# A whole network in one kernel: the first branches re-ordered with one logarithm, output projections taken by pairs of blocks, and priorities for the conformer's statistics

## The chip, the cores and the metric

The kernel runs on one core of a Trainium2 chip. The metric is the device time of one execution in microseconds (us). A core has five engines that each work through their own queue in order: TensorE (PE; its weight loads are shown apart as PEld), VectorE (DVE), ScalarE (ACT), GpSimd (POOL) and SyncE (SP), which here issues DMA transfers.

## The reference

One sequence of 256 tokens with 1024 features goes through two hybrid layers and then through a second stack: mixer, attention, FFN, conformer, attention, FFN. What is computed in the places of the change:

```python
def hybrid_layer(...):                       # twice, l = 0 and 1
    h = rms_norm(x, norm_pre);  proj = h @ w_in
    # sb_*, ml_*, gm_*, rt_*, xa_* and the gates are column blocks of proj
    y_sb = stick_breaking(sb_q, sb_k, sb_v)  # below
    q_ml = silu(causal_conv(ml_q, conv_q))   # k_ml likewise
    h_ml = mlstm(q_ml, k_ml, ml_v, ml_i + b_igate, ml_f + b_fgate)
    ...                                      # three more branches
    merged = sum(sigmoid(gates) * up(ys))
    return x + rms_norm(merged @ w_out, norm_post)

def stick_breaking(q, k, v):                 # by blocks of 128 queries, 4 heads
    z = q @ k.T * scale;  valid = key_pos < q_pos
    log_keep = where(valid, -softplus(z), 0)
    later = reverse_cumsum(log_keep) - log_keep
    return where(valid, exp(log_sigmoid(z) + later), 0) @ v

x = x + mixer_ab(x)      # ... concatenate([y_a, y_b]) @ w_out
x = x + cross_attn(x, mem, 0);  x = x + conv_ffn(x, 0)
def conformer_conv(x):
    h = glu(rms_norm_2(x) @ w1 + b1);  h = causal_dwconv(h, dw_w, dw_b)
    return silu(layer_norm_2(h)) @ w2 + b2
x = x + conformer_conv(x)
x = x + cross_attn(x, mem, 1);  x = x + conv_ffn(x, 1)
return rms_norm_2(x, final_norm)
```

## The kernel before, in words

Activations lie with features on partitions, in blocks of 128x256. Every matrix product is made in float32 from two halves, high and low: `wh*xh + wh*xl + wl*xh`. The weights stream from HBM in tiles of 512 KB (`weights`, L274 on): SP loads a tile `raw`, ScalarE rounds it to `wh` (L289), VectorE subtracts for `wl` (L290), and TensorE reads both. `raw` has five buffers, `wh` and `wl` four, so the conversion of a tile waits until TensorE is done with one four tiles back.

Three helpers issue the products. `mm_F` (L294) makes a feature-major block; its tiles in PSUM are named psF, or psO in an output projection. It goes over its 128-column blocks and, in each, over the four k-blocks of two weight tiles. `mm_T` makes token-major tiles psT, `proj_P` tiles psP. One weight tile is worth 24 matmuls of 128x256. `proj_F` (L339) calls `mm_F` in two steps of four k-blocks and may run a function `mid` between them.

A norm is applied late: `Norm.pair` adds squares (`sqacc`, L213 to L226) while it splits x into `xhl`; `column` sums over partitions with the matmul ps_ss (L169), `row_of` turns the result with ps_rb (L182) into a row that scales later outputs.

The order of a hybrid layer: projections sb_q and sb_k, with the statistic between; `blocks` makes the logits z of three blocks in turn, and `got` takes each at once through Exp (L557), Ln (L558), mask, and the halves sb_sp (L565, L566). Then sb_v, the gates' columns (`gates_if`), and sb_z, in whose middle `later` runs: eight matmuls ps_later (L578), Exp, mask on POOL (L583). After sb_z, `silu2_F` scales with a tanh (sbz_t, L385, L386), and ps_sbo (L595 to L599) multiplies with the values. The rotary table (`early[0]`: ang, rot_k, sinF, cosF, L471 to L499) and `ml_branch` follow: ps_gt and gi (L623) give the input and forget gates, `softplus_neg_abs` (L188) a polynomial of tiny steps, ps_rows (L633, L634) turns them to rows, a scan gives mlrows (L638 to L641), then ps_cols (L646, L647) and ps_m (L655).

An output projection (psO) makes two halves of 512 columns; each half takes all its k-blocks before the next half begins. `add_to_x` (L967) adds psO to x, after which the next `Norm.pair` splits (L246, L247).

In the conformer (`conformer`, L1099) the layer norm subtracts a mean (L1165), adds squares, gets its row `cln_rb` in the middle of the value projection of the next attention (v_2, psT), scales (L1176), applies Silu (L1180), and splits to `yhl` (L241, L242), which psO reads.

The program's text does not set the order by itself: a scheduler places instructions on each engine by when their inputs are there and by priorities (`tc.high_priority(offset=...)`, and `issue_after`), once, when the program is built. Each engine then runs its list in order.

## Time and profile before

| | |
|---|---|
| device time, median of 3 runs | 1792.82 us (1791.99 to 1793.71) |
| profiled execution | 1790.47 us, its span 1788.8 us |
| TensorE busy | 1760.0 us, 98% of the span |
| weight loads of TensorE | 1593.7 us, 89% |
| VectorE busy | 1291.1 us, 72% |
| ScalarE busy | 997.4 us, 56% |
| GpSimd busy | 47.4 us, 3% |
| DMA | 309.94 MB, mean 173 GB/s |

The span is what the profiler sees between the first and the last instruction; the profiled execution's own time has 1.7 us around it. Busy shares are means over stages with different limits. With TensorE at 98%, the rest is read from the places where it waits. A wait is shown with the engine and instruction that ended it.

### The profile page before, as it was taken

Reading aid. Unit: us, or ns where it says so; the run is one execution under the profiler, and the core shown is the slowest. Engines: PE = TensorE matmul, PEld = TensorE weight load, DVE = VectorE, ACT = ScalarE, POOL = GpSimd, SP = SyncE. Lnnn points to the kernel's source line nnn. Section 1 sums busy time; section 2 is a strip of 40 time slices with the busy share of each in tenths; the row PEclk is TensorE's granted clock in tenths of the full one; section 3 lists DMA queues with packets and bytes.
Section 4 is the critical chain, followed back from the end, with each engine's and each line's share of the span. In section 5 each row is a group of like instructions: output and inputs, shape, how many; then the busy total and the mean of one; then the engine's idle time right before and its main releaser. Section 6 shows DMA issues by size and latency. Waiting matters only on the chain.

```text
span 1788.8 us, 28271 instructions
## 1 busy us (share of the span) xinstructions
PE 1760.0 (98%) x11082; PEld 1593.7 (89%) x11082; DVE 1291.1 (72%) x1965; ACT 997.4 (56%) x1479; POOL 47.4 (3%) x68
## 2 busy tenths in 40 slices
PE   8899999999999999999999999999999999999998
PEld 8889998888999898888899999999999989998886
DVE  5887855676657877566657975687779996587866
ACT  5755345554556543556455855565558545466654
POOL 1010000000001100000000000000000000000000
PEclk9999999999999999999999999999999999999999
DMA  7457465666555655567655454556564344466563
GB/s 237 127 191 234 150 188 157 195 213 189 166 167 158 188 175 159 157 193 244 204 172 182 148 179 151 157 184 189 179 194 142 103 134 144 133 186 189 181 193 102
DMA packets 186806, 309.94 MB, mean 173 GB/s; under 512 B 10576, under 2 KB 68048, under 8 KB 186672
## 3 DMA queue, kind: packets, MB, share of 16 engines
q1 hardware_dynamic: 184304, 302.04, 53.8%
q0 software_dynamic: 1360, 5.05, 0.9%
q8 instruction: 87, 1.43, 0.3%
q10 hardware_dynamic: 1008, 1.05, 0.2%
q14 instruction: 47, 0.39, 0.1%
HBM read 307.04 MB, written 1.05 MB: 172 GB/s over the span
## 4 chain that ended last, share of the span: by engine, by line
PE 83%; DVE 7%; issue 6%; ACT 3%; DMA 1%; POOL 0%; SPq 0%; POOLq 0%; DVEq 0%; ACTq 0%
PE psT L336 26%; PE psF L302 20%; PE psO L302 11%; PE psP L316 10%; PE psP L318 5%; PE psO L336 4%; DVE c_h L1144 3%; DVE wl L290 2%; PE ps_lg L924 1%; PE ps_xo L1221 1%; ACT wh L289 1%; PE ps_blk L419 1%; DMA raw<-in_w_in 1%; PE ps_pT L943 0%; PE ps_xo L852 0%
## 5 line engine op out<-in xcount | busy, mean ns | idle before, releaser
L290 DVE TENSOR_TENSOR wl<-raw,wh 128x1024 fp32r<-128x1024 f32 x556 | 670.0, 1222 | 328.1 <-ACT wh L289 318.3
L289 ACT ACTIVATE wh<-raw 128x1024 fp32r<-128x1024 f32 x556 | 576.9, 1056 | 514.7 <-PE psT L336 164.0
L302 PE MATMUL psF<-xhl,wh 128*128 128x256 f32 x2176 | 400.9, 286 | 0.2 <-DVE a_z L363 0.2
L302 PEld LDWEIGHTS psF<-xhl,wh 128*128 128x128 f32 x2176 | 342.9, 193 | 2.0 <-issue 0.7
L336 PE MATMUL psT<-wh,xhl 128*128 128x512 f32 x1088 | 337.3, 391 | 0.0
L302 PE MATMUL psF<-xhl,wl 128*128 128x256 f32 x1088 | 310.1, 285 | 0.0
L316 PE MATMUL psP<-xhl,wh 128*128 128x512 f32 x768 | 271.2, 398 | 0.0
L336 PEld LDWEIGHTS psT<-wh,xhl 128*128 128x128 f32 x1088 | 203.2, 188 | 41.2
L302 PE MATMUL psO<-yhl,wh 128*128 128x256 f32 x1216 | 222.8, 286 | 4.4 <-ACT yhl L241 4.4
L318 PE MATMUL psP<-xhl,wl 128*128 128x256 f32 x768 | 214.4, 280 | 0.0
L336 PE MATMUL psT<-wl,xhl 128*128 128x512 f32 x544 | 212.9, 391 | 0.0
L302 PEld LDWEIGHTS psF<-xhl,wl 128*128 128x128 f32 x1088 | 209.9, 193 | 0.5 <-issue 0.3
L302 PEld LDWEIGHTS psO<-yhl,wh 128*128 128x128 f32 x1216 | 191.2, 193 | 5.2 <-ACT yhl L241 4.8
L316 PEld LDWEIGHTS psP<-xhl,wh 128*128 128x128 f32 x768 | 144.3, 188 | 34.5
L302 PE MATMUL psO<-yhl,wl 128*128 128x256 f32 x608 | 173.0, 285 | 0.9 <-DVE wl L290 0.9
L318 PEld LDWEIGHTS psP<-xhl,wl 128*128 128x128 f32 x768 | 144.9, 189 | 0.2
L336 PEld LDWEIGHTS psT<-wl,xhl 128*128 128x128 f32 x544 | 102.2, 188 | 21.0
L302 PEld LDWEIGHTS psO<-yhl,wl 128*128 128x128 f32 x608 | 117.0, 192 | 1.1 <-DVE wl L290 1.1
L336 PE MATMUL psT<-wh,yhl 128*128 128x512 f32 x320 | 98.5, 389 | 0.0
L336 PEld LDWEIGHTS psT<-wh,yhl 128*128 128x128 f32 x320 | 60.1, 188 | 12.5
L302 PE MATMUL psF<-mhl,wh 128*128 128x256 f32 x384 | 70.1, 284 | 0.0
L1144 DVE SCALAR_TENSOR_TENSOR c_h<-c_a,cols,c_h 128x228 f32<-128x228 f32 (+16 forms) x144 | 63.3, 464 | 3.0
(395 smaller groups left out, 2084.0 us busy)
## 6 DMA issues: line engine op xcount, KB each, us to landing
raw<-in_w_in SPq DMA_DIRECT2D x224, 512.0 KB, 4.5
raw<-in_f_w_up SPq DMA_DIRECT2D x96, 512.0 KB, 3.8
raw<-in_f_w_down SPq DMA_DIRECT2D x48, 512.0 KB, 4.3
raw<-in_w_up SPq DMA_DIRECT2D x40, 512.0 KB, 4.4
raw<-in_c_w_pw SPq DMA_DIRECT2D x24, 512.0 KB, 4.4
raw<-in_ab_w_in SPq DMA_DIRECT2D x20, 512.0 KB, 4.3
raw<-in_w_mem_kv SPq DMA_DIRECT2D x16, 512.0 KB, 4.5
raw<-in_w_out SPq DMA_DIRECT2D x16, 512.0 KB, 4.0
```

Of the source, the lines that this page charges most:

```text
L289: A.activation(hi, raw, AF.Copy)
L290: V.tensor_tensor(lo, raw, hi.bitcast(F32), op=ALU.subtract)
L302: PE.matmul(pss[m // 2][:, m % 2], a, b, start=(first and m % 2 == 0 and k == 0 and n == 0), stop=(last and k == n_k - 1 and n == 2), skip ...
L316: PE.matmul(pss[m], wh, op.hl[:, k0 + k], start=(k0 + k == 0), stop=False, skip_group_check=True)
L318: PE.matmul(pss[m][:, 0], wl, op.h[:, k0 + k], start=False, stop=(k0 + k == 7), skip_group_check=True)
L336: PE.matmul(pss[t], a, b, start=(first and k == 0 and n == 0), stop=(last and k == n_k - 1 and n == 2), skip_group_check=True)
L419: PE.matmul(ps[:, h], kF[:, h, s * 128:s * 128 + 128], qF[:, h, t * 128:t * 128 + 128], start=(h == 0), stop=True, skip_group_check=True)
L924: PE.matmul(pl[:, t], q[:, t * 128:t * 128 + 128], k, start=(t == 0 and n == 0), stop=(n == len(pairs) - 1), skip_group_check=True)
L1144: V.scalar_tensor_tensor(h[:, j:], a[:, m, 0:S - j], col("c_dw_w_2", (30 - j) * 8 + c), h[:, j:], op0=ALU.mult, op1=ALU.add)
L1221: PE.matmul(po[:, dj], vT[i][:, m, c0:c0 + 128], pT[:, m], start=(dj == 0 and m == 0), stop=(m == 1), skip_group_check=True)
```

## The change

- `proj_F` can work in steps of two k-blocks (one weight tile) and run functions between them. In layer 0 the statistic's column is taken after the first weight tile of sb_k, its row after the second. In layer 1 the column is taken ahead of sb_k. In the opening the last squares get a priority of 200.
- Stick-breaking takes all three blocks through Exp, then one Ln over all of them (128x1536), then the masks and halves. The rotary table is made between that and sb_v.
- `sb_out` (ps_sbo and what follows) becomes a function that `ml_branch` calls after the ml_q convolution.
- `proj_out` makes output projections by pairs of k-blocks: one weight tile for the first half of the columns, one for the second, and so on. It serves the w_out of both layers, mixer ab, both attentions and the conformer.
- In the conformer, the subtraction of the mean and the squares get a priority of 900, the scaling, Silu and split one of 300; a Silu over 128x8 is added (c_early); the column and the row are taken one step of two k-blocks earlier.

```diff
@@ -336,13 +336,16 @@
                     PE.matmul(pss[t], a, b, start=(first and k == 0 and n == 0),
                               stop=(last and k == n_k - 1 and n == 2), skip_group_check=True)
 
-    def proj_F(w, c0, op, n_k=8, n=512, mid=None, get=None):
+    def proj_F(w, c0, op, n_k=8, n=512, mid=None, get=None, mids=None):
         pss = [(get or mbank)([128, 2, S], "psF") for _ in range(n // 256)]
-        for k0 in range(0, n_k, 4):
-            if k0 and mid:
+        step = 2 if mids else 4
+        for k0 in range(0, n_k, step):
+            if k0 == 4 and mid:
                 mid()
-            mm_F(pss, w[k0 * 128:(k0 + 4) * 128, c0:c0 + n], op, k0, 4, k0 == 0,
-                 k0 + 4 >= n_k)
+            if mids and k0 in mids:
+                mids[k0]()
+            mm_F(pss, w[k0 * 128:(k0 + step) * 128, c0:c0 + n], op, k0, step, k0 == 0,
+                 k0 + step >= n_k)
         return pss
 
     def proj_T(w, c0, op, n_k=8, mid=None, mids=None):
...
@@ -505,9 +508,14 @@
         stage("layer" if l else "start")
         pss_q = made.pop() if made else proj_F(w, OFF["sb_q"], op)
         stage("layer")
-        rc, row = nrm.column(), []
-        pss_k = proj_F(w, OFF["sb_k"], op, mid=lambda: row.append(row_of(rc, "x")))
-        rb = row[0]
+        row = []
+        if l:
+            row.append(nrm.column())
+        mids = {4: lambda: row.append(row_of(row[0], "x"))}
+        if not l:
+            mids[2] = lambda: row.append(nrm.column())
+        pss_k = proj_F(w, OFF["sb_k"], op, mids=mids)
+        rc, rb = row
         pins.clear()
 
         bif = t_sm([128, 2, 4], "bif")
...
@@ -549,13 +557,16 @@
             kF = F_plain(w, OFF["sb_k"], op, rb, "sbk", pss=pss_k)
             zs = t_f6([128, 3, NH, 128], "sb_zs")
             sps = {}
+            abs3 = t_f6([128, 3, NH, 128], "sb_abs")
 
             def got(b, ps):
+                ab = abs3[:, b]
                 A.activation(zs[:, b], ps, AF.Copy, scale=128.0 ** -0.5)
-                ab = t_f4([128, NH, 128], "sb_abs")
                 V.scalar_tensor_tensor(ab, zs[:, b], -1.0, zs[:, b], op0=ALU.mult, op1=ALU.max)
                 A.activation(ab, ab, AF.Exp, scale=-1.0)
-                A.activation(ab, ab, AF.Ln, bias=1.0)
+
+            def keep(b):
+                ab = abs3[:, b]
                 V.scalar_tensor_tensor(ab, zs[:, b], 0.0, ab, op0=ALU.max, op1=ALU.add)
                 if b != 1:
                     G.affine_select(ab, ab, pattern=[[0, NH], [1, 128]],
...
@@ -567,6 +578,10 @@
                 sps[b] = sp
 
             blocks(kF, qF, got)
+            A.activation(abs3, abs3, AF.Ln, bias=1.0)
+            for b in range(3):
+                keep(b)
+            early[0]()
             vT = T_plain(w, OFF["sb_v"], op, rc, "sbv")
             gates_if()
             def later():
...
@@ -586,6 +601,9 @@
 
             pss_z = proj_F(w, OFF["sb_z"], op, mid=later)
             z = silu2_F(w, OFF["sb_z"], op, rb, "sbz", pss=pss_z)
+            return lambda: sb_out(zs, vT, z)
+
+        def sb_out(zs, vT, z):
             o = Operand(4, yop, "y")
             for i in range(2):
                 ps = bank([128, 2, S], "ps_sbo")
...
@@ -615,7 +633,7 @@
             V.scalar_tensor_tensor(c, th, 1.0, c, op0=ALU.add, op1=ALU.mult)
             return c
 
-        def ml_branch():
+        def ml_branch(rest):
 
             ps = gate_sums()
             gi = t_sm([128, 2, 8], "gi")
...
@@ -664,6 +682,7 @@
                 G.affine_select(dm[:, b], dm[:, b], pattern=[[0, NH], [1, 128]],
                                 compare_op=ALU.is_ge, fill=0.0, base=0, channel_multiplier=-1)
             qF = conv_silu2(OFF["ml_q"], "conv_q", "mlq")
+            rest()
             kF = conv_silu2(OFF["ml_k"], "conv_k", "mlk")
 
             def got(b, p):
...
@@ -857,9 +876,7 @@
                 o.put_scaled(sl, z[:, sl], 0.5)
             ys[4] = o
 
-        sb_branch()
-        early[0]()
-        ml_branch()
+        ml_branch(sb_branch())
         early[1]()
         ws = gm_weights()
         gm_branch(ws)
...
@@ -960,6 +974,14 @@
                     mids=mids)
         ahead[0] = was
         return v
+
+    def proj_out(pss, w, parts):
+
+        steps = [(o, kp, r0 + 256 * kp) for o, r0 in parts for kp in range(2)]
+        for n, (o, kp, r) in enumerate(steps):
+            for cg in range(2):
+                mm_F(pss[cg], w[r:r + 256, cg * 512:cg * 512 + 512], o, 2 * kp, 2, n == 0,
+                     n == len(steps) - 1)
 
     def out_banks():
         return [[mbank([128, 2, S], "psO") for _ in range(2)] for _ in range(2)]
...
@@ -1091,9 +1113,7 @@
         yas.append(gated(1, h1))
         wo = I["ab_w_out_2"][0]
         pss = out_banks()
-        for n, (o, r0) in enumerate(((yas[0], 0), (yb, D), (yas[1], 512))):
-            for cg in range(2):
-                mm_F(pss[cg], wo[r0:r0 + 512, cg * 512:cg * 512 + 512], o, 0, 4, n == 0, n == 2)
+        proj_out(pss, wo, [(yas[0], 0), (yb, D), (yas[1], 512)])
         return add_to_x(pss, Norm(*nxt))
 
     def conformer(nrm, ks, vs, nxt):
...
@@ -1159,34 +1179,35 @@
 
         ks.append(k_2(1, 1, mean))
         s2 = Sq()
-        for h in outs:
-            for i in range(2):
-                hh = h[:, 2 * i:2 * i + 2]
-                V.tensor_tensor(hh, hh, bc(mb, 2), op=ALU.subtract)
-                s2.add(hh)
+        with tc.high_priority(offset=900):
+            for h in outs:
+                for i in range(2):
+                    hh = h[:, 2 * i:2 * i + 2]
+                    V.tensor_tensor(hh, hh, bc(mb, 2), op=ALU.subtract)
+                    s2.add(hh)
         got = []
-        vs.append(v_2(1, 0, mids={4: lambda: got.append(s2.column("cln")),
-                                  6: lambda: got.append(row_of(got[0], "cln"))}))
+        early = t_sm([128, 8], "c_early")
+        A.activation(early, s2.acc[:, 0:8], AF.Silu)
+        vs.append(v_2(1, 0, mids={2: lambda: got.append(s2.column("cln")),
+                                  4: lambda: got.append(row_of(got[0], "cln"))}))
         lb = got[1]
         ops = []
         for i, h in enumerate(outs):
             o = Operand(4, yop, "y")
             for m2 in range(2):
                 sl = slice(2 * m2, 2 * m2 + 2)
-                V.tensor_tensor(h[:, sl], h[:, sl], bc(lb, 2), op=ALU.mult)
-                for j in range(2):
-                    m = 2 * m2 + j
-                    c = 4 * i + m
-                    A.activation(h[:, m], h[:, m], AF.Silu, scale=col("c_ln_g_2", c),
-                                 bias=col("c_ln_b_2", c))
-                o.put(sl, h[:, sl])
+                with tc.high_priority(offset=300):
+                    V.tensor_tensor(h[:, sl], h[:, sl], bc(lb, 2), op=ALU.mult)
+                    for j in range(2):
+                        m = 2 * m2 + j
+                        c = 4 * i + m
+                        A.activation(h[:, m], h[:, m], AF.Silu, scale=col("c_ln_g_2", c),
+                                     bias=col("c_ln_b_2", c))
+                    o.put(sl, h[:, sl])
             ops.append(o)
         pss = out_banks()
         w2 = I["c_w_pw2_2"][0]
-        for n, o in enumerate(ops):
-            for cg in range(2):
-                mm_F(pss[cg], w2[n * 512:n * 512 + 512, cg * 512:cg * 512 + 512], o, 0, 4, n == 0,
-                     n == 1)
+        proj_out(pss, w2, [(o, n * 512) for n, o in enumerate(ops)])
         return add_to_x(pss, Norm(*nxt), "c_b_pw2_2")
 
     def cross_attn(l, nrm, kF, vT_fn, nxt):
...
@@ -1348,7 +1366,8 @@
     opening.__exit__(None, None, None)
     pins += [last_hi.ins, last_lo.ins]
     with tc.issue_after(last_hi.ins), tc.issue_after(last_lo.ins):
-        nrm.sq.add(xF[:, 6:8])
+        with tc.high_priority(offset=200):
+            nrm.sq.add(xF[:, 6:8])
         load_cols(nc.scalar, 8, base["ab_norm_2"])
         load_cols(nc.scalar, base["ab_norm_2"], n_cols)
     mem = {}
```

The w_out of the layers and the output projection of `cross_attn` are replaced in the same way.

The lists that the scheduler makes of this, at three places. First, ScalarE's list in layer 0, from the logits on (sb_zs and sb_abs are the logits and their softplus, sb_sp its high half, sbv the values, g_rows the gates' columns, L289 a weight tile). Before:

```order
L554 ACTIVATE sb_zs<-ps_blk 128x512 x3
L557 ACTIVATE sb_abs<-sb_abs 128x512
L558 ACT_TABLE_LOAD
L558 ACTIVATE sb_abs<-sb_abs 128x512
L565 ACTIVATE sb_sp<-sb_abs 128x512
L289 ACTIVATE wh<-raw 128x1024
L557 ACT_TABLE_LOAD
L557 ACTIVATE sb_abs<-sb_abs 128x512
L289 ACTIVATE wh<-raw 128x1024
L558 ACT_TABLE_LOAD
L558 ACTIVATE sb_abs<-sb_abs 128x512
L565 ACTIVATE sb_sp<-sb_abs 128x512
```
Now, with the line numbers of the changed kernel (L566 is the Exp, L581 the Ln, L576 the copy to sb_sp, L499 the sine):

```order
L564 ACTIVATE sb_zs<-ps_blk 128x512 x3
L566 ACTIVATE sb_abs<-sb_abs 128x512 x3
L581 ACT_TABLE_LOAD
L581 ACTIVATE sb_abs<-sb_abs 128x1536
L499 ACT_TABLE_LOAD
L499 ACTIVATE sinF<-rot_r 128x256
L289 ACTIVATE wh<-raw 128x1024 x2
L576 ACTIVATE sb_sp<-sb_abs 128x512 x3
L381 ACTIVATE sbv<-psT,x_rc 128x512
L289 ACTIVATE wh<-raw 128x1024 x2
L381 ACTIVATE sbv<-psT,x_rc 128x512
```
Of the loads of an activation table, five for Exp and Ln (three of them shown) become one, that of the sine stands earlier, the weight tiles' conversions stand behind the logarithm, and all three sb_sp are together.

Second, TensorE's list in layer 0 around the gates' matmuls ps_cols and ps_m, in the ml_q projection (psF). Before:

```order
L302 MATMUL psF<-xhl,wl 128x256
L302 MATMUL psF<-xhl,wh 128x256 x2
L655 MATMUL ps_m<-mlrows,ident 128x256 x3
L647 MATMUL ps_cols<-ident,mlrows 128x4
L646 MATMUL ps_cols<-ident,mlrows 128x4
L647 MATMUL ps_cols<-ident,mlrows 128x4
L655 MATMUL ps_m<-mlrows,ident 128x256
L302 MATMUL psF<-xhl,wl 128x256
L302 MATMUL psF<-xhl,wh 128x256 x2
```
Now (L613 to L617 are ps_sbo):

```order
L302 MATMUL psF<-xhl,wl 128x256
L302 MATMUL psF<-xhl,wh 128x256
L673 MATMUL ps_m<-mlrows,ident 128x256 x4
L613 MATMUL ps_sbo<-sb_zs,sbv 128x128
L665 MATMUL ps_cols<-ident,mlrows 128x4
L664 MATMUL ps_cols<-ident,mlrows 128x4
L665 MATMUL ps_cols<-ident,mlrows 128x4
L615 MATMUL ps_sbo<-sb_zs,sbv 128x128
L617 MATMUL ps_sbo<-sb_zs,sbv 128x128
L613 MATMUL ps_sbo<-sb_zs,sbv 128x128
```
The matmuls ps_sbo, which stood ahead of ps_gt, are here, behind ps_m. Of psF, 38 stand between ps_gt and the first ps_rows (26 before), then 45 to the other three ps_rows (69), 17 to the first ps_cols (31) and 12 to ps_m (8). In layer 1 the last three are 51, 20 and 12.

Third, ScalarE's list in the conformer (cln_rb is the layer norm's row, vT the values, c_h the activations). Before:

```order
L218 ACTIVATE sq<-c_h 128x512
L289 ACTIVATE wh<-raw 128x1024 x3
L185 ACTIVATE cln_rb<-ps_rb 128x256
L378 ACTIVATE vT<-psT,mem_rc 128x512
L1180 ACT_TABLE_LOAD
L1180 ACTIVATE c_h<-c_h,cols 128x256
L289 ACTIVATE wh<-raw 128x1024
L378 ACTIVATE vT<-psT,mem_rc 128x512
L1180 ACTIVATE c_h<-c_h,cols 128x256 x2
L241 ACTIVATE yhl<-c_h 128x2x256
L1180 ACTIVATE c_h<-c_h,cols 128x256 x2
L241 ACTIVATE yhl<-c_h 128x2x256
```
Now (L1204 is the Silu, L1190 the added one):

```order
L215 ACTIVATE sqacc<-c_h 128x512
L218 ACTIVATE sq<-c_h 128x512 x3
L289 ACTIVATE wh<-raw 128x1024 x3
L1190 ACT_TABLE_LOAD
L1190 ACTIVATE c_early<-sqacc 128x8
L289 ACTIVATE wh<-raw 128x1024
L185 ACTIVATE cln_rb<-ps_rb 128x256
L289 ACTIVATE wh<-raw 128x1024
L1204 ACTIVATE c_h<-c_h,cols 128x256 x8
L241 ACTIVATE yhl<-c_h 128x2x256 x4
L289 ACTIVATE wh<-raw 128x1024
L381 ACTIVATE vT<-psT,mem_rc 128x512 x2
```
The table load moves ahead of cln_rb, one more weight conversion comes between cln_rb and the first Silu, all eight Silu stand together ahead of the first yhl, and the copies of vT are behind. On TensorE, 19 psT stand ahead of ps_ss, 6 more ahead of ps_rb, and 23 between that and psO (25, 11 and 12 before).

## Rows read from the trace of the kernel before

**Rows 1.** The page's busy times, shares and instructions of each engine.
```profile
PE 1760.0 (98%) x11082; PEld 1593.7 (89%) x11082; DVE 1291.1 (72%) x1965; ACT 997.4 (56%) x1479; POOL 47.4 (3%) x68
```

**Rows 2.** Waits of TensorE: engine line waited for, us in total, times, longest.
```profile
PE ps_rows L633 <- DVE gi L623: 2.6, 1, 2.6
PE ps_ss L169 <- DVE sqacc L223: 2.0, 1, 2.0
PE ps_later L578 <- ACT sb_sp L565: 1.2, 2, 0.6
PE ps_later L578 <- DVE sb_sp L566: 1.0, 2, 0.7
PE ps_sbo L599 <- POOL sb_zs L583: 0.9, 1, 0.9
PE ps_sbo L595 <- POOL sb_zs L583: 0.5, 1, 0.5
PE ps_cols L646 <- DVE mlrows L639: 0.3, 1, 0.3
```

**Rows 3.** Windows: stretch, length, busy time and instructions per engine, granted clock, DMA.
```profile
23.50:26.90 3.40, 3.40 (x19) 3.40 (x18) 0.00 (x0) 0.00 (x0) 1.11 (x2) 0.51 1.04 355
566.20:569.70 3.50, 3.50 (x18) 3.50 (x18) 1.85 (x4) 3.50 (x11) 1.82 (x3) 0.51 0.82 255
1479.00:1484.40 5.40, 5.32 (x23) 5.16 (x24) 2.77 (x4) 4.16 (x9) 0.00 (x0) 0.50 0.30 97
1485.00:1500.00 15.00, 15.00 (x127) 15.00 (x127) 7.30 (x10) 7.06 (x9) 0.00 (x0) 1.00 0.43 140
```

**Rows 4.** Timeline, VectorE, the first statistics: start, us, what [idle before].
```profile
21.15 0.43 DVE L223 TENSOR_TENSOR sqacc<-sqacc,sq 128x256 f32<-128x256 f32 x1
...
492.17 0.41 DVE L223 TENSOR_TENSOR sqacc<-sqacc,sq 128x256 f32<-128x256 f32 x1
```

**Rows 5.** Timeline, layer 0, ps_later and the last sb_sp: TensorE and ScalarE.
```profile
56.11 1.09 PE L578 MATMUL ps_later<-sb_sp,tri_ones 128*128 128x512 f32 x4
...
57.12 0.63 ACT L565 ACTIVATE sb_sp<-sb_abs 128x512 fp32r<-128x512 f32 x1 [0.25 <-POOL sb_abs L561]
...
59.02 0.96 PE L578 MATMUL ps_later<-sb_sp,tri_ones 128*128 128x512 f32 x3 [0.72 <-DVE sb_sp L566]
```

**Rows 6.** Timeline, layer 0, before the gates' rows: ScalarE and VectorE.
```profile
71.36 1.28 ACT L385 ACT_TABLE_LOAD   x1
...
73.75 1.23 DVE L386 SCALAR_TENSOR_TENSOR sbz<-sbz_t,sbz 128x1024 f32<-128x1024 f32 x1 [0.96 <-ACT sbz_t L385]
...
76.21 0.22 DVE L623 SCALAR_TENSOR_TENSOR gi<-gsum,x_rc,bif 128x8 f32<-128x8 f32 x1
```

**Rows 7.** Timeline, TensorE, start of mixer ab's output projection.
```profile
1032.09 0.40 PE L302 MATMUL psO<-yhl,wh 128*128 128x256 f32 x2
...
1034.82 0.38 PE L302 MATMUL psO<-yhl,wl 128*128 128x256 f32 x1 [0.89 <-DVE wl L290]
```

**Rows 8.** Timeline, conformer, before its second projection: ScalarE, then TensorE.
```profile
1471.34 1.06 ACT L289 ACTIVATE wh<-raw 128x1024 fp32r<-128x1024 f32 x1 [2.11 <-PE psT L336]
...
1474.11 1.28 ACT L1180 ACT_TABLE_LOAD   x1
...
1477.43 1.08 ACT L1180 ACTIVATE c_h<-c_h,cols 128x256 f32<-128x256 f32 x2
1478.41 0.62 ACT L241 ACTIVATE yhl<-c_h 128x512 fp32r<-128x512 f32 x1
1479.08 1.31 PE L302 MATMUL psO<-yhl,wh 128*128 128x256 f32 x4 [4.36 <-ACT yhl L241]
```

**Rows 9.** Timeline, VectorE, end of attention 0's output projection.
```profile
1136.31 2.35 DVE L290 TENSOR_TENSOR wl<-raw,wh 128x1024 fp32r<-128x1024 f32 x2
1138.58 0.87 DVE L247 SCALAR_TENSOR_TENSOR xhl<-xF,cols,xhl 128x256 fp32r<-128x256 f32 x2
...
1141.47 0.69 DVE L972 TENSOR_TENSOR xF<-xF,psO 128x512 f32<-128x512 f32 x1 [0.81 <-PE psO L302]
```

10 lines of the change are left out of this document (2 added, 8 removed).

## The prediction

> **What bounds the kernel now.** I read the page's busy times first. TensorE is busy for 1760.0 of 1788.8 us [rows 1], so the weight conversions on ScalarE and VectorE, the DMA and every table load cost time only where TensorE waits for them. The next view is therefore the list of TensorE's waits: what the reader is to see is that a handful of single waits, each under 5 us, holds all that can be won by re-ordering [rows 2]. The windows with the granted clock come third: in three places the clock is near half (1.2 instead of 2.4 GHz) for some microseconds [rows 3]. At full clock a 128x256 matmul follows the last every 0.12 us: 15.00 us over the 127 of the fourth window, two taken off for its edges. In the slow windows the same division gives 3.4/17 = 0.20, 3.5/16 = 0.22 and 5.4/21 = 0.26 (a few records are missing). I take 0.215, so a slow stretch loses 44% of itself: 1.5 us, 1.5 us and 2.4 us. The timelines around each wait come last.
>
> The profiled execution took 1790.47 us: its span of 1788.8 and 1.7 around it. It lies 2.35 below the median of 1792.82; the sum is made against 1790.47, and 2.35 is added back at the end.
>
> **The change part by part.** A wait costs its idle time and some 0.15 us for filling the pipeline again; I use start to start where rows give it.
>
> 1. *Layer 0, first statistic.* The matmul ps_ss stands behind 24 psF of the first K weight tile instead of 7, so TensorE comes to it 17 x 0.12 = 2.04 us later. It idled 2.0 us for the last sum of squares [rows 2], which ended at 21.58 [rows 4]. So it meets it with at most 0.15 to wait even if nothing else were earlier, and the two squares of the last columns are given priority besides: 2.0 gained. Behind this wait the clock fell (first window of [rows 3]); with the wait gone I take the 1.5 us as gained too. From none to all of it: 2.0 to 3.5. I take 3.5, since nothing else interrupts TensorE there. The next waiter would be ps_rb, now behind 48 psF, 24 x 0.12 = 2.9 us after ps_ss; it needs one VectorE and one ScalarE step. No wait.
>
> 2. *Layer 0, stick-breaking.* Exp, load, Ln, load, alternately for three blocks, becomes three Exp, one load, one Ln over 1536 columns: ScalarE loses four loads of 1.28 us each (the price of a load is in [rows 6]), 5.1 us, and the long Ln saves two starts. The last sb_sp was ready at 57.65, its low part later [rows 5]; it now stands some ten instructions earlier in both queues, about 46.5 by adding the durations, and TensorE is there at 52 to 53. The five ps_later matmuls from 56.11 to 59.02 took 2.91 us; at the 0.233 of the first four, (1.09 - 0.39)/3, they need 1.17. Gained 1.75, nothing if the new chain were 6 us longer than I add up. What it delays is the sine and cosine and one weight tile's conversion, both with microseconds of cover.
>  The page "ScalarE: Activation LUTs" of the Trainium skill says under "Table sets: the hidden batching unit" that one set holds exp and ln, so that going from one to the other needs no second load. This trace differs: L557 and L558 each load a table in turn, and the list of the changed kernel still has one load for the Ln. By the page steps 2 and 5 would be worth only the shorter queue, 0 to 1 us instead of 3.
>
> 3. *Layer 0, ps_sbo.* It waited 0.5 and 0.9 us for POOL's masks [rows 2], with two refills 1.7. Its 12 matmuls now stand behind the whole ml_q projection, 15 us later, where the masks are long done. Gained 1.7. The adds of ps_sbo to sbz move with it, and yhl of this branch comes later; it is not read before the end of the layer.
>
> 4. *Layer 0, gates.* ps_rows waited 2.6 us for gi [rows 2] (2.8 start to start). The chain: Tanh load to 72.64, Tanh, L386 from 73.75 to 74.98, two adds of ps_sbo, gi to 76.43 [rows 6]. After the change the Sin is loaded once and early, no load stands ahead of the Tanh but that of Exp, and the adds are behind gi: 1.28 x 2 + 1.28 off the chain. But ps_rows' three later matmuls, ps_cols and ps_m come after only 45, 17 and 12 psF (69, 31 and 8 before), and in VectorE's order two weight conversions of 1.22 us stand between the steps of the softplus. Adding up both queues, I find new waits of 0.2 to 0.6 each at ps_rows, ps_cols and ps_m, 1.1 together: gained 1.7. Bounds: all 2.8 gone, or a second wait as long as the first behind each of two conversions (2.8 - 2 x 1.9 = -1.0).
>
> 5. *Layer 1, ps_later.* Of the idle time under that name [rows 2] 2.2 - 1.3 = 0.9 belongs to layer 1; with two refills 1.3, gained as in 2. Layer 1's statistic moves ahead, to directly behind the last matmul of the stage before; its squares end at 492.58 [rows 4], before TensorE gets there, so no wait.
>
> 6. *Layer 1, gates.* Before, the list has 0.3 at ps_cols [rows 2], some 0.9 start to start with the small waits below the list's grain; the shorter fillers of step 4 apply here too (51, 20 and 12 psF). I add up two waits of about 0.7, 1.4 in all: lost 0.5. The half clock after ps_m (second window of [rows 3]) can stay, go, or appear in layer 0 as well: +-1.5, taken as 0.
>
> 7. *Mixer ab, output projection by pairs.* psO began at 1032.09 and stood still for 0.89 until 1034.82 for the low part of the second weight tile [rows 7]. By pairs, the second tile is needed after all 24 matmuls of the first, at 1032.09 + 2.88 = 1034.97. Gained 1.0.
>
> 8. *Conformer.* psO waited 4.36 us [rows 8]: rb, four multiplications, table load, Silu between weight conversions, first yhl at 1478.41. Now ps_rb stands 11 matmuls of 128x512 earlier, 2.6 us at the 0.233 of step 2, and the load is done before it. But ScalarE's order puts one more weight conversion before the first Silu, and that waits for TensorE to free its buffer (as the one at 1471.34 did); I add up 1472.95 for its end. All eight Silus, 0.5 us apart (1.08 for two [rows 8]), stand before the first yhl: 1472.95 + 4.0 + 0.6 = 1477.6 against 1479.08. Gained 1.5; about 3 us of gap stay, and so most likely does the half clock behind it, from which I take 0.5 for the shorter gap: 2.0 in all, from 1.5 to 6.9 (wait and half clock both gone, third window of [rows 3]).
>
> 9. *Ends of the paired projections.* With pairs the first half of the output is complete 24 matmuls, 2.88 us, before the end, instead of 48 or 5.76. At four ends (mixer to attention 0, attention 0 to ffn 0, conformer to attention 1, attention 1 to ffn 1) the next stage reads columns that come from adds and splits queued behind pairs of weight conversions: 2.35 us, then 0.87 for two splits, and the last add waited 0.81 for psO [rows 9]. TensorE did not wait there before. I add up up to 0.45 us late at one end, less at others: lost 1.0, bounds 0 and 4 x 3.2 (a pair of conversions and the splits ahead of every end). I take the low value, since the splits of the first columns are still in time at all four when I add up the queue.
>
> Sum: 3.5 + 1.75 + 1.7 + 1.7 + 1.3 - 0.5 + 1.0 + 2.0 - 1.0 = 11.5 gained. 1790.47 - 11.5 = 1779.0; with 2.35, 1781.3 us.
>
> **The rivals.**
> A, the gate chains and the conformer give nothing: steps 4, 6 and 8 come to -2.0 instead of +3.2. For it speaks that both orders put conversions inside the chain, and the 11.5 is mostly small terms; against it that the loads are off. 11.5 - 5.2 = 6.3: 1786.5.
> B, the conformer's wait and half clock go entirely: 4.9 more, 1776.4. For it: the load of 1.28, the second conversion and the vT copy leave the chain. Against it: eight Silus and a conversion ahead of the first yhl. What the half clock hangs on is open in the trace: an idle gap of 2.0 had one behind it, one of 2.6 had none [rows 2, 3].
>  The page "TensorE: Matmul & The Clock Gate" of the Trainium skill asks, under "Why this matters for your kernels", to leave no long idle gap between bursts of matmuls. By it the shortened gap would be the better half of B, 2.4 us; the trace agrees only in part, as the 2.0 and 2.6 show.
> C, slower: every paired end pays. At each of the four the first add stands behind two weight conversions (2.35), the split follows (0.87), and the interruption brings a half clock (1.5): 4.7 x 4 = 18.9 against 12.5 from the other steps, 6.4 lost: 1799.2. It decides from 12.5/4 = 3.1 us an end. Against it: VectorE sat idle 0.81 just there [rows 9], and only two of the four have all these in a row.
> D, the waits only move: the chains off TensorE are shorter, but the next consumer waits instead, and gains and losses cancel: 1789 to 1794, say 1792. Against it: for steps 1 to 3 the next consumer stands 2.9 us of matmuls or more behind.
>
> **How the numbers follow.** Forecast 0.50, A 0.22, B 0.13, D 0.10, C 0.05. Its own range is 1778 to 1785; down to B and up to between A and D, the range is 1775 to 1790. Under 0.2% (3.6 us) a run of this kernel cannot be told from no change: faster means below 1789.2, slower above 1796.4. Forecast, B and nearly all of A are faster, 0.83; D and the edge of A are the same, 0.12; C is slower, 0.05.
>
> **What would show it.** In the profile after: no wait of ps_ss, ps_later and ps_sbo over 0.3 us (1, 2, 3, 5); no half clock at 23 us; Silu's load before cln_rb and psO waiting about 3 us (8); no wait of psO for wl in the mixer (7); waits below 0.5 at the first matmuls after each paired end (9). The prediction fails if the gates wait longer than before, or if TensorE waits behind the paired ends for splits for more than 1 us each.

## The result, and the profile after

| | before | after |
|---|---|---|
| device time, median | 1792.4 us (1788.6 to 1793.7, 4 runs) | 1783.5 us (1782.7 to 1784.5, 4 runs) |
| ratio to before | | 0.9949, 95% interval 0.9937 to 0.9960 |
| profiled execution, its span | 1790.47, 1788.8 us | 1784.10, 1782.4 us |

The kernel became 0.5% faster, 8.9 us in the medians where 11.5 were forecast, and inside the range (1775 to 1790). The two profiled executions lie 6.4 us apart: the forecast put the second at 1779.0, and it took 1784.10. The page of the changed kernel gives TensorE one per cent more of a shorter span [rows 1]:

```profile
PE 1758.7 (99%) x11082; PEld 1591.0 (89%) x11082; DVE 1294.7 (73%) x1965; ACT 987.2 (55%) x1466; POOL 51.3 (3%) x68
```

The list of TensorE's waits after the change, those that are new or that the prediction spoke of (left out are waits that stood there before as well, such as warm 2.2 us, ps_conv 1.3 and ps_rb 0.9):

```profile
PE ps_blk L422 <- DVE sbk L366: 3.2, 1, 3.2
PE psO L302 <- ACT yhl L241: 2.7, 1, 2.7
PE psO L302 <- DVE a_z L366: 0.9, 1, 0.9
PE psP L316 <- DVE xF L994: 0.7, 2, 0.3
PE ps_ss L169 <- DVE sqacc L223: 0.5, 2, 0.3
PE ps_cols L664 <- DVE mlrows L657: 0.4, 2, 0.2
```

Against [rows 2], ps_rows, ps_later and ps_sbo are gone, and ps_ss has only two short waits left, in the layers' closing norms. New are ps_blk, a_z and psP. To see what each place gained, I took the time from start to start of every matmul above the steady pitch (0.12 us for 128x256, 0.227 for 128x512) from the timelines. The time that the half clock (1.2 GHz, about 0.21 us for a 128x256 matmul) costs is in it:

| place (us above the pitch) | before | after | forecast gain | measured |
|---|---|---|---|---|
| 1 layer 0, first statistic | 3.9 | 0.1 | 3.5 | 3.8 |
| layer 0, ps_blk (new) | 0.2 | 3.5 | 0 | -3.3 |
| 2 layer 0, ps_later | 1.9 | 0 | 1.75 | 1.9 |
| 3 layer 0, ps_sbo | 2.2 | 0.3 | 1.7 | 1.9 |
| 4 layer 0, gates | 3.9 | 3.2 | 1.7 | 0.7 |
| 5 layer 1, ps_later | 1.4 | 0 | 1.3 | 1.4 |
| 6 layer 1, gates | 3.3 | 1.9 | -0.5 | 1.4 |
| both layers, ps_num (new) | 0.6 | 1.3 | 0 | -0.7 |
| 7 mixer, psO | 1.2 | 1.1 | 1.0 | 0.1 |
| 8 conformer, psO | 7.3 | 5.3 | 2.0 | 2.0 |
| 9 ends of paired projections | 0 | 2.0 | -1.0 | -2.0 |
| statistics at the layers' ends | 2.3 | 2.8 | 0 | -0.5 |
| whole program | 68.7 | 62.0 | 11.5 | 6.7 |

The windows with the granted clock: at the gates of layer 0, of layer 1, and behind the conformer's wait. The half clock is no longer in layer 1 [rows 3] but in layer 0, and behind the conformer's wait it is shorter.

```profile
80.00:83.50 3.50, 3.50 (x18) 2.93 (x17) 2.83 (x8) 3.05 (x9) 0.15 (x2) 0.58 0.77 240
552.00:563.00 11.00, 10.80 (x80) 9.59 (x80) 10.12 (x23) 7.05 (x16) 0.15 (x2) 1.00 0.62 188
1472.00:1476.00 4.00, 3.43 (x16) 3.22 (x17) 3.65 (x5) 3.96 (x7) 0.00 (x0) 0.65 0.04 15
```

The new wait of layer 0, VectorE and then TensorE. `ang`, the cast of the positions, sits ahead of sbk and waits 3.35 us for its transfer, which ScalarE's queue had issued at 25.60:

```profile
27.26 1.28 DVE L366 TENSOR_TENSOR sbq<-psF,x_rb 128x512 f32<-128x512 f32 x2
31.90 0.29 DVE L479 CAST ang<-pos_i 128x256 f32<-128x256 int32 x1 [3.35 <-DMA pos_i<-in_positions]
...
33.96 0.69 DVE L366 TENSOR_TENSOR sbk<-psF,x_rb 128x512 f32<-128x512 f32 x1
34.70 2.94 PE L422 MATMUL ps_blk<-sbq,sbk 128*128 128x128 f32 x24 [3.16 <-DVE sbk L366]
```

The conformer on ScalarE, which answers to [rows 8]: row, one weight conversion that waits for TensorE, eight Silus, the splits. The Silus end at 1471.77, so the first split (1471.68) starts as the last Silu drains:

```profile
1464.46 0.39 ACT L185 ACTIVATE cln_rb<-ps_rb 128x256 f32<-128x256 f32 x1
1466.76 1.06 ACT L289 ACTIVATE wh<-raw 128x1024 fp32r<-128x1024 f32 x1 [1.92 <-PE psT L336]
1467.73 4.04 ACT L1204 ACTIVATE c_h<-c_h,cols 128x256 f32<-128x256 f32 x8
1471.68 2.19 ACT L241 ACTIVATE yhl<-c_h 128x512 fp32r<-128x512 f32 x4
```

Mixer ab, VectorE and TensorE [rows 7]: the wait for the low part of the second weight tile has become one for a_z, whose scaling frees the PSUM banks of the second half and stands behind three weight conversions:

```profile
1027.20 3.49 DVE L290 TENSOR_TENSOR wl<-raw,wh 128x1024 fp32r<-128x1024 f32 x3
1030.61 0.69 DVE L366 TENSOR_TENSOR a_z<-psF,x_rb 128x512 f32<-128x512 f32 x1
1031.44 0.47 PE L302 MATMUL psO<-yhl,wh 128*128 128x256 f32 x2 [0.86 <-DVE a_z L366]
```

End of attention 0's projection [rows 9]: the matmul psP waits for the last add of psO, since that add frees its banks; the add stands behind a weight conversion:

```profile
1139.93 1.22 DVE L290 TENSOR_TENSOR wl<-raw,wh 128x1024 fp32r<-128x1024 f32 x1
...
1141.40 0.68 DVE L994 TENSOR_TENSOR xF<-xF,psO 128x512 f32<-128x512 f32 x1
1142.23 0.47 PE L316 MATMUL psP<-xhl,wh 128*128 128x512 f32 x1 [0.33 <-DVE xF L994]
```

### The profile page after: what moved, and what is told of

The parts are those of the page before. It is cut to its first block, busy times and chain, and to the rows that moved or that the text cites. A ratio compares the mean times of both kernels' runs of the same rounds, so it can differ in the third digit from the quotient of the medians.

```text
span 1782.4 us, 28259 instructions
## 1 busy us (share of the span) xinstructions
PE 1758.7 (99%) x11082; PEld 1591.0 (89%) x11082; DVE 1294.7 (73%) x1965; ACT 987.2 (55%) x1466; POOL 51.3 (3%) x68
## 4 chain that ended last, share of the span: by engine, by line
PE 84%; DVE 8%; issue 6%; ACT 2%; DMA 1%; POOL 0%; POOLq 0%; SPq 0%; DVEq 0%; ACTq 0%
PE psT L336 28%; PE psF L302 20%; PE psO L302 10%; PE psP L316 10%; PE psP L318 5%; PE psO L336 4%; DVE c_h L1164 3%; DVE wl L290 2%; PE ps_lg L938 1%; PE ps_blk L422 1%; PE ps_xo L1242 1%; ACT wh L289 1%; PE psF L1362 1%; PE ps_pT L957 0%; PE ps_xo L871 0%
## 5 line engine op out<-in xcount | busy, mean ns | idle before, releaser
L289 ACT ACTIVATE wh<-raw 128x1024 fp32r<-128x1024 f32 x556 | 580.8, 1058 | 542.0 <-PE psT L336 171.6
L336 PEld LDWEIGHTS psT<-wh,yhl 128*128 128x128 f32 x320 | 60.1, 188 | 12.5
```

The source lines that it names most:

```text
L289: A.activation(hi, raw, AF.Copy)
L336: PE.matmul(pss[t], a, b, start=(first and k == 0 and n == 0), stop=(last and k == n_k - 1 and n == 2), skip_group_check=True)
```

## The experiments

Each experiment changes the kernel after the change, unless another is named; device times are medians of 4 to 11 runs. The diffs show only the lines that matter. The changed kernel was timed in one sitting, the experiments in three later ones. The kernel before, timed in each, had medians of 1792.4, 1792.4, 1793.4 and 1792.8 us, so a difference of 1 to 2 us between two medians is not resolved by itself.

**e_cast: the cast of the positions behind sbk.**

```diff
+        with tc.issue_after(scaled[0].ins):   # the scaling of sb_k
-        V.tensor_copy(ang, pi)
+            V.tensor_copy(ang, pi)
```

> The changed kernel, with one edit: the cast of the positions (first step of the rotary table, L479) may be placed on VectorE only behind the scaling of sb_k. Theory: the new wait of 3.3 us at ps_blk in layer 0 comes from this cast, which stands ahead of sbk in VectorE's list and waits for its own DMA of 6.3 us; then the wait at ps_blk falls from 3.2 to under 0.8 us and the kernel is 2.5 to 3.3 us faster than the changed kernel (about 1780.5). Rival: the row of the statistic and the two halves of sb_k simply come too late, since both halves end together now; then ps_blk still waits 1.5 us or more and at most 1.5 us are gained. Second rival: the wait moves to the next reader, ps_later or the gates, and the time stays at 1783.5.

Measured: 1779.4 us (1777.5 to 1782.5), 4.1 us below the changed kernel. VectorE's timeline has both halves of sbk and only then the cast, without a wait; TensorE does not wait for sbk any more, and the third row, the window over the gates of layer 0, shows full clock:

```profile
30.66 1.46 DVE L368 TENSOR_TENSOR sbk<-psF,x_rb 128x512 f32<-128x512 f32 x2
32.03 0.28 DVE L482 CAST ang<-pos_i 128x256 f32<-128x256 int32 x1
70.00:81.00 11.00, 10.84 (x80) 9.59 (x80) 10.46 (x25) 7.44 (x17) 0.15 (x2) 1.00 0.58 183
```

The theory holds. The new wait was the cast. The profiled executions lie 4.7 us apart: 3.3 at ps_blk, and 1.5 because the half clock at the gates is gone although their waits are unchanged; why stays open.

**e_stat: the statistic where it was before.**

```diff
-        pss_k = proj_F(w, OFF["sb_k"], op, mids=mids)   # column after 24 psF, row after 48
+        rc, row = nrm.column(), []
+        pss_k = proj_F(w, OFF["sb_k"], op, mid=lambda: row.append(row_of(rc, "x")))
```

> The changed kernel with the statistic of both layers put back where it was before (ps_ss after 7 psF of sb_k, ps_rb in its middle, steps of four k-blocks); all else as changed. Theory (step 1 of the prediction was right in what it removed): ps_ss waits about 2 us again and the clock falls behind it for 3.4 us, 3.5 us in all; the cast of the positions still stands between the two halves of sbk, so ps_blk still waits, 0 to 3 us. In all 0.5 to 3.5 us slower than the changed kernel. Rival: the later statistic itself made the wait at ps_blk, so undoing it takes 3.3 away and gives 3.5 back: no difference, 1783.5, with no wait at ps_blk.

Measured: 1782.6 us (1779.8 to 1784.4), not told apart from the changed kernel; the theory's loss did not come. The wait of ps_ss is back (1.9 of these 2.4 us are layer 0's), with the half clock behind it, and that of ps_blk is gone, as the rival said. The second row is the cast, which now waits for nothing:

```profile
PE ps_ss L169 <- DVE sqacc L223: 2.4, 3, 1.9
32.95 0.28 DVE L479 CAST ang<-pos_i 128x256 f32<-128x256 int32 x1
```

The number is the rival's, its reason is not: e_cast kept the later statistic and lost the wait. VectorE comes to the cast at 32.95 here, behind TensorE's wait and half clock, and came at 28.5 in the changed kernel. The positions landed at 32.7 here (issued at 29.1) and at 31.9 there (issued at 25.6): the transfer lands at nearly the same time, and an engine that arrives sooner waits for it.

**e_early: the rotary table back behind the branch.**

```diff
-            early[0]()                 # between keep(b) and sb_v
+        rest = sb_branch()
+        early[0]()
+        ml_branch(rest)
```

> The changed kernel with the first half of the rotary table (early[0]) put back behind the stick-breaking branch. Theory: no wait at ps_blk (the cast is far behind), 3.3 us gained there; given back in part, since the sine and the cosine load their table each for itself and stand in the chain ahead of the gates again: waits of ps_rows 1 to 2.5 us. In all 1 to 2.5 us faster than the changed kernel. Rival (the row of the statistic makes the wait): ps_blk still waits 1.5 us or more, and with the gates' wait back the kernel is 0 to 2 us slower.

Measured: 1781.4 us (1779.8 to 1781.7), 2.1 us faster, with all five runs below the four of the changed kernel. No wait at ps_blk, and one of 1.4 us at the gates in its place, both as the theory had it:

```profile
PE ps_rows L650 <- DVE gi L640: 1.4, 1, 1.4
```

**e_perblock: Exp and Ln block by block.**

```diff
-            A.activation(abs3, abs3, AF.Ln, bias=1.0)      # one for three blocks
+                A.activation(ab, ab, AF.Ln, bias=1.0)      # in got(b), ab = abs3[:, b]
```

> The changed kernel with Exp and Ln taken block by block again (27 table loads instead of 23, three Ln loads ahead of sb_sp in layer 0 where there is one), all else as changed, the early rotary table and the placing of the three blocks' masks among it. Theory of the prediction's step 2 as it was written: four loads off ScalarE are what made sb_sp early; then ps_later waits again, 1.7 us in layer 0 and 1.3 in layer 1, and the kernel is 2 to 3 us slower than the changed one. Rival: the order of the whole branch does it, sb_sp was 5 us ahead of ps_later, and two more loads (2.6 us) still fit; then no wait at ps_later and the same time as the changed kernel within 1 us.

Measured: 1785.1 us (1779.9 to 1787.1), not told apart from the changed kernel: both are 0.995 of the kernel before timed beside them. First the changed kernel, then this one: the end of the copies to sb_sp on ScalarE, and ps_later on TensorE.

```profile
46.19 1.66 ACT L576 ACTIVATE sb_sp<-sb_abs 128x512 fp32r<-128x512 f32 x3
...
55.77 2.03 PE L593 MATMUL ps_later<-sb_sp,tri_ones 128*128 128x512 f32 x8
```

```profile
49.94 0.62 ACT L574 ACTIVATE sb_sp<-sb_abs 128x512 fp32r<-128x512 f32 x1
...
57.19 2.03 PE L588 MATMUL ps_later<-sb_sp,tri_ones 128*128 128x512 f32 x8
```

Ready at 47.85 and 50.56, read from 55.77 and 57.19. ps_later waits in neither. The median is 1.6 us higher; in the profiled execution a half clock of 3.4 us at 35 us that the other had not costs 1.7. The rival holds: two of the four loads can come back, and ps_later does not wait. The one logarithm by itself is not what freed it.

**e_perf4: e_perblock, with a tile for each block as before.**

```diff
-                ab = abs3[:, b]
+                ab = t_f4([128, NH, 128], "sb_abs")
```

> e_perblock with one more step back: each block's softplus lies in a tile of its own from the pool of nine buffers that the rest of the branch uses (as before), instead of in one tile for three blocks. In ScalarE's list Exp and Ln alternate again with a load each and the sb_sp stand apart. Theory: the storage is what bound the blocks one behind the other; ps_later waits again, 1 to 2 us in layer 0 and up to 1.3 in layer 1, and the kernel is 1.5 to 3.5 us slower than e_perblock, leaving the half clock aside. Rival: the early rotary table and the rest of the order keep sb_sp early enough; no wait at ps_later.

Measured: 1789.1 us (1786.8 to 1791.4), 4.0 us slower than e_perblock, a little more than the theory's 3.5. ps_later waits in both layers, and ps_blk much less than in e_perblock (3.0); the last sb_sp of layer 0 is ready at 58.2:

```profile
PE ps_later L587 <- ACT sb_sp L573: 2.5, 2, 2.1
PE ps_later L587 <- DVE sb_sp L574: 0.5, 2, 0.2
PE ps_blk L422 <- DVE sbk L366: 0.4, 1, 0.4
...
57.60 0.63 ACT L573 ACTIVATE sb_sp<-sb_abs 128x512 fp32r<-128x512 f32 x1 [1.20 <-POOL sb_abs L569]
```

So the storage sets the order, and the order brings the wait. With a tile of its own for each block the scheduler sets Exp and Ln alternately, and the sine and the cosine, each with a load, between them: seven loads and four weight conversions stand between the logits and the last sb_sp. With one tile for three blocks and three Ln it is three loads and two conversions. From the last copy of the logits to the last sb_sp ScalarE takes 20.6 us here and 10.9 in e_perblock; the four loads are 5.1 of these 9.7. Whether the loads or the rest of the order would have been enough alone is not shown. Nor are the 4.0 us this wait alone: between the two profiled executions, 4.2 apart, the two places of ps_later cost 5.0 us more start to start, and the way to ps_later in layer 0 costs 2.5 less.

**e_sbo: ps_sbo at the end of its branch again.**

```diff
-            return lambda: sb_out(zs, vT, z)
+            sb_out(zs, vT, z)
+            return lambda: None
```

> The changed kernel with ps_sbo called at the end of the stick-breaking branch again, all else as changed. Theory (step 3): ps_sbo waits for POOL's masks again, 1.7 us in layer 0, and the adds of ps_sbo stand ahead of gi again, so ps_rows waits up to 1.3 us; 1.7 to 3 us slower than the changed kernel. Rival: with the table loads gone the masks are done earlier and ps_sbo meets them; then 0 to 0.5 us.

Measured: 1783.5 us (1781.2 to 1786.1), the same. POOL's two masks end at 61.00 and ps_sbo starts at 62.88; ps_rows does not wait either. The third row, the window behind the conformer's wait of 2.7 us, is at full clock where the changed kernel, with the same wait, had 0.65:

```profile
58.69 2.31 POOL L598 TENSOR_SCALAR_AFFINE_SELECT sb_zs<-sb_zs 128x512 f32<-128x512 f32 x2 [13.44 <-ACT sb_zs L596]
...
62.88 0.39 PE L614 MATMUL ps_sbo<-sb_zs,sbv 128*128 128x128 f32 x2
...
1470.70:1476.00 5.30, 5.01 (x39) 4.81 (x40) 4.33 (x6) 4.66 (x8) 0.00 (x0) 1.00 0.07 11
```

The rival holds: with the masks early, the later place of ps_sbo brings nothing.

**e_conf: the conformer as before, pairs kept.**

```diff
-        with tc.high_priority(offset=900):     # subtraction and squares
-        A.activation(early, s2.acc[:, 0:8], AF.Silu)
-        mids={2: ..., 4: ...}                  # column, row
+        mids={4: ..., 6: ...}
-                with tc.high_priority(offset=300):   # scaling, Silu, split
```

> The changed kernel with the conformer's statistics, scaling and Silu as before (no priorities, no early table load, column and row one step later), the paired output projection kept. Theory (step 8): psO waits 4.4 us instead of 2.7 and the half clock behind it is 6.8 us long instead of 3.4; 1.5 to 3 us slower than the changed kernel. Rival: the pairs alone shortened both, since only two column blocks of yhl are needed at first; then under 1 us.

Measured: 1787.5 us (1783.9 to 1788.1), 4.0 us slower. The wait is back at its old length, so the pairs alone do not shorten it:

```profile
PE psO L302 <- ACT yhl L241: 4.4, 1, 4.4
```

Which of the parts undone together (priorities, early load, earlier column and row) had shortened the wait is not shown. The size is less clear than the sign. The theory's half clock of 6.8 us did not come: behind the wait there is one stretch of 3.4, as in the changed kernel. The profiled execution (1783.86) is the fastest of the five and no longer than the changed kernel's. ps_blk waits 0.6 in it, since TensorE's first matmuls ran at the slow pitch until 11.3 us (until 7.2 in the changed kernel) and VectorE came to the cast later. The other four runs (1786.4 to 1788.1) had a mean clock of 0.994 to 0.996 where the changed kernel had 0.997. The wait is 1.7 us longer, 1.1 start to start with the half clock behind it; that the rest of the 4.0 us is the clock is likely by the slope in the last section, and not traced.

**e_chain: e_cast, with two Silus and a split at a time.**

```diff
+                    held.enter_context(tc.issue_after(a.ins))   # a: the high half of this split;
+                    # what the loop issues next stands behind it
```

> The changed kernel with the cast of the positions late (as in e_cast) and, in the conformer, each pair of Silus held back until the split of the pair before is issued, so that the first yhl stands behind two Silus instead of eight. Theory: the wait of psO in the conformer is the eight Silus; the first yhl comes some 2 us earlier (two Silus and a copy of vT ahead of it), the wait falls from 2.7 to about 0.9 us, and with so short a gap the half clock goes or stays at 3.4 us: 1.8 to 3.5 us faster than e_cast (1779.4), about 1777. Rival: the following column blocks come too late instead (each needs two Silus and a split, 1.6 us, against 5.8 us of matmuls for each pair of k-blocks), and the time stays at 1779.4.

Measured: 1777.3 us (1775.5 to 1778.4), 2.1 us below e_cast; the profiled executions lie 3.9 apart. ScalarE, TensorE, and the window over the conformer's second projection:

```profile
1461.98 1.06 ACT L289 ACTIVATE wh<-raw 128x1024 fp32r<-128x1024 f32 x1 [1.89 <-PE psT L336]
1462.95 1.08 ACT L1207 ACTIVATE c_h<-c_h,cols 128x256 f32<-128x256 f32 x2
1463.93 0.67 ACT L383 ACTIVATE vT<-psT,mem_rc 128x512 f32<-128x512 f32 x1
1464.50 0.62 ACT L1210 ACTIVATE yhl<-c_h 128x512 fp32r<-128x512 f32 x1
1465.17 1.12 PE L302 MATMUL psO<-yhl,wh 128*128 128x256 f32 x4 [0.33 <-ACT yhl L1210]
1462.00:1492.00 30.00, 29.56 (x233) 28.55 (x232) 20.21 (x28) 20.33 (x31) 0.00 (x0) 1.00 0.58 177
```

The wait is 0.33 us and the clock behind it is full. In rows of 4 us this is the one kernel in which no stretch from 2 to 1766 us is shown below 1.00.

**e_nopairs: output projections half by half.**

```diff
-        for n, (o, kp, r) in enumerate(steps):      # 256 rows at a time
+        for n, (o, r) in enumerate(parts):          # 512 rows, then the other columns
```

> The changed kernel with all output projections as before (each half of the columns through all k-blocks), all else as changed. Theory: the pairs cost more than they bring: the waits at the four ends (0.3, 0.6, 0.3, 0.6 us start to start) go, 1.5 us in all; in mixer ab the wait of 1.0 us for a_z, which frees the banks of the second half, turns back into the wait of 1.1 us for the low part of the second weight tile; in the conformer the first matmuls need four column blocks of yhl instead of two, 0 to 0.7 us more. In all 0.8 to 1.8 us faster than the changed kernel (about 1782.3). Rival: the pairs are what shortened the conformer's wait and its half clock; then the conformer loses 1.5 us or more and the kernel is not faster.

Measured: 1782.3 us (1779.5 to 1784.0), 1.2 us below the changed kernel's median and inside the scatter of both. What the pairs cost is better read from the profiles. Start to start it has 60.1 us above the pitch where the changed kernel has 62.0: the four ends and the layers' closing norms give 2.8, the mixer nothing (the wait for wl, below, in place of that for a_z), the conformer loses 0.9 to a longer half clock at the same wait:

```profile
PE psO L302 <- DVE wl L290: 0.9, 1, 0.9
PE psO L302 <- ACT yhl L241: 2.7, 1, 2.7
```

**e_best: e_chain, pairs in the conformer and the mixer alone, a_z first.**

```diff
-        proj_out(pss, w, parts)                     # layers, attentions: half by half
+            with tc.high_priority(offset=300):
+                scaled_F(pss_z, rb, z)              # a_z
```

> e_chain with two more edits. Pairs of k-blocks stay only in the conformer and in mixer ab; the w_out of the layers and the attentions' output projections are made half by half again. In mixer ab the scaling of a_z, which frees the banks that the second half of psO needs, gets a priority of 300 over the weight conversions. Theory: the wait of psO in mixer ab (0.9 us idle, 1.1 start to start) goes, since the second weight tile is needed only after 2.9 us and the banks are free by then; the two waits of psP for the last add of psO (0.6 each start to start) go; the waits at the first statistics of the layers fall by 0.1 to 0.2 each. In all 2.0 to 2.8 us faster than e_chain (1777.3), about 1775. Rival: with a_z scaled earlier the weight conversion behind it is late, and psO waits for wl in its place; then only the 1.2 to 1.6 us of the attentions are gained.

Measured: 1775.6 us (1774.6 to 1776.4; ratio to the kernel before 0.9908, 0.9895 to 0.9922), 1.7 us below e_chain and the lowest median of all; the ratio of e_chain to the kernel before beside it is 0.9907, so the two are not told apart. psP no longer waits. In the mixer the rival was right: a_z is scaled at 1022.51, early enough, and psO waits for the weight conversions that moved behind it and the scans:

```profile
PE psO L302 <- DVE wl L290: 0.8, 1, 0.8
1022.51 0.67 DVE L368 TENSOR_TENSOR a_z<-psF,x_rb 128x512 f32<-128x512 f32 x1
1024.86 3.49 DVE L290 TENSOR_TENSOR wl<-raw,wh 128x1024 fp32r<-128x1024 f32 x3
```

## Why the prediction came out as it did

The sum was 11.5, the measured gain 8.9 in the medians and 6.4 to 6.7 between the profiled executions; the sum was made against the first of these. The forecast's direction and range held; its reasons held in part. That the medians came within 2.2 us of the forecast (1783.5 for 1781.3) is partly luck: the profiled execution missed it by 5.1 (1784.10 for 1779.0), through losses of 3.3 at ps_blk and 2.0 at the paired ends of which the sum had only 1.0, and the median runs gained more in mean clock (0.994 to 0.997) than the two profiles (0.995 to 0.997).

- Step 1 was right in what it removed (3.8) and failed where it said that "nothing else interrupts TensorE there". The chain behind the statistic was read for ps_rb and no further; the cast and its transfer, moved by step 2 ahead of sbk, were not followed. Nearly the whole gain of the step went back there: 3.3 us, shown by e_cast.
- Step 2 and step 5 have the right size (1.9 and 1.4), and the loads are only a part of the cause. The time 46.5 for the last sb_sp was 1.3 early (47.85), with ps_later at 55.77 still far behind. Two of the four loads back do not bring the wait back (e_perblock); the alternating order does, with seven loads in it (e_perf4), and the loads are 5.1 of the 9.7 us by which it is longer. "What it delays is the sine and cosine ..., both with microseconds of cover" missed that the rotary table is also placed ahead of other work.
- Step 3: the wait went (1.9), but not by the later place of ps_sbo: e_sbo has it in the old place without a wait. The masks, which ended at 67.8 before and at 61.5 after, came early with the new order of step 2; that was not tested by itself.
- Steps 4 and 6 were forecast at 1.7 and -0.5 and measured 0.7 and 1.4, together 2.1 for 1.2. Without the half clock, which was in layer 1 before and in layer 0 after (about 1.6 each), the stages have 1.6 and 1.9 after the change; the forecast of 1.1 and 1.4 was a little low. The gains are then 2.3 and -0.2; the half clock alone made step 6 a gain.
- Step 7 failed: that the wait for wl would go was right, but the next late thing was not looked for. The banks of the second half are needed 2.9 us earlier by pairs, and a_z holds them. Gained 0.1 for 1.0.
- Step 8 was right: 2.0 forecast and measured, the wait with eight Silus in a row 1.6 us shorter and the half clock shorter. e_conf shows that the conformer's edits shortened the wait and not the pairs, e_chain that the order of Silus and splits makes what was left.
- Step 9 was mis-sized: 2.0 for 1.0. At the two ends of the attentions it is not the splits but the last add, which frees psO's banks. Its wait of 0.81 for psO [rows 9] was read as slack; by pairs a weight conversion took the slack and the add came behind it. At the other two ends (0.3 each) the profile names no wait.

The signs that the prediction named came true, all of them: no wait of ps_ss, ps_later and ps_sbo over 0.3, no half clock at 23 us, psO at 2.7, none for wl, waits of 0.33 behind the attentions. They asked whether the old waits were gone, and none asked what stood in their place.

Rival A is refuted: steps 4, 6 and 8 gave 4.1 and not -2.0. Rival B's larger gain at the conformer did not come with this change, but came with e_chain. Rival C's mechanism is there at a tenth to a quarter of the price from which it would decide (0.3 to 0.8 us an end against 3.1), and without a half clock behind it. Rival D, that the waits only move, was refuted as a whole but is what happened in steps 1 and 7: 3.3 of 3.8 went to ps_blk, 1.1 of 1.2 to a_z. What spoke against it for step 1 took ps_rb for the next consumer; the one that waited was ps_blk.

The rule of the Trainium skill on one set for exp and ln ("ScalarE: Activation LUTs", "Table sets: the hidden batching unit") brings no saving in these traces: e_perblock, with three blocks stored together, still has a load at each change between L566 and L567 (1.28 us each, at 40.76, 43.23 and 45.17). Which set a load brings they do not show. The rule of the Trainium skill in "TensorE: Matmul & The Clock Gate" ("Why this matters for your kernels") to avoid long idle gaps fits e_chain, whose gap is 0.33 and whose clock stays full, but the gap of 2.7 had a half clock behind it in the changed kernel and none in e_sbo.

## What to carry to other kernels

When a statistic, a row or a table is moved, follow every instruction that it issues, the small transfers too, to the place where each now stands in an in-order queue: a cast of 0.29 us held the engine for 3.35. And let the signs of a forecast ask for new waits as well as for old ones. When a wait is costed at its full length, look for what is late next at that very place: a buffer or a PSUM bank is as good a reason as an operand. And undo parts one at a time: here the later statistic and the later ps_sbo, undone alone, changed nothing, the early rotary table cost 2.1 us, the pairs cost some 2 by the profile, the conformer's part gained, and the one logarithm worked through the order that one tile for three blocks gave.

## What the runs showed of the hardware

Runs of one kernel differ by several microseconds with the granted clock. Of the kernel before, timed beside the last experiments:

```
device us   mean granted clock
1788.50     0.996
1790.35     0.995
1792.49     0.994
1794.10     0.993
```

That is 1.9 us for each 0.001. Windows of 4 us over the profiled executions show where it comes from: the clock is full except in single stretches of some 3.4 us at half clock. Counted in that way there are four in the kernel before (at 23, 567 and, two on end, 1479 us), two in the changed one (80 and 1473), one in e_cast (1469), none in e_chain, one in e_best (79), one in e_sbo (85), two in e_early and e_conf, three in e_stat, e_nopairs and e_perblock, four in e_perf4. The first microseconds and the last few are left out: every kernel shows the half clock at its end, and its first matmuls follow each other at the slow pitch of 0.21 us up to 7 or 8 us, in e_conf and e_perf4 up to 11.3 and 11.8, although the column says 1.00 there.

Where TensorE works through a stretch, it loses 1.4 to 1.7 us start to start. The pair at 1479 begins at 1478 within the wait, and that part costs nothing. In all, the stretches lose some 5.4 us in the kernel before and 3.3 in the changed one: about 2 of the 6.4 us between the two profiled executions are the clock, about 4 are shorter waits. The median runs lie at a clock of about 0.994 before, 0.997 after and 0.998 with e_chain. By the slope 5 to 6 of the 8.9 us would go with it, which is too much: the same slope gives 3.7 between the profiled executions, where it is about 2. How the 8.9 us divide is thus known only roughly.

A wait is worth more than its length where a stretch follows it. Which wait is followed by one is not settled: at the same place, behind the same wait of 2.7 us, five kernels had one (the changed one, e_cast, e_stat, e_early, e_perblock), two had two (e_nopairs, e_perf4) and one had none (e_sbo). And the stretch at 80 us of the changed kernel has no idle time over 0.2 us in the 4 us ahead of it, only the small matmuls ps_cols and ps_m.

The transfer of the positions (128 KB, one row copied to all partitions) took 6.3 us from issue to landing in the changed kernel, 3.7 in e_conf, 5.7 in e_sbo, and 3.0 in the kernel before. But it was issued at 25.6, 27.4, 25.7 and 29.2 us, and so landed at 31.9, 31.1, 31.4 and 32.2. In all twelve profiles it landed between 30.8 and 32.7, whether it was issued at 25.5 or at 29.2. What holds it until then is not shown; the DMA engines were busy for 0.73 to 0.77 of the time from 24 to 32 us in the changed kernel. So the wait at ps_blk is not a fixed price either: it is the time by which VectorE comes too soon, 3.2 us in the changed kernel's profile, 0.4 to 3.1 in those of the experiments that left that stage as it was.
